# Sums of the activations for the Strassen-like gate products: taken from the x of the q and k stage instead of loaded again per head

## The chip, the cores and the metric

One core of a Trainium2 chip. The metric is the device time of one execution in microseconds; the median of several runs is compared. The engines' names here are those of the profile: PE is TensorE's matrix multiplication and PEld its weight load, DVE is VectorE, ACT is ScalarE, POOL is GpSimd, SP is SyncE, whose queue issues most of the DMAs.

## What is computed

One layer of an encoder trunk, 512 positions of width 1024, all in float32. The part that matters here is the first half:

```python
h = rmsnorm(x, g_pre_mix)                       # (512, 1024)
q, k, v, g, u, sv, a_ret, a_sgu = split(h @ w_in, ...)
y_ret = (layernorm(retention(rotary(q), rotary(k), v)) * silu(g)) @ w_ret_o   # 4 heads, both directions
y_sgu = (gelu(u) * (w_spatial . layernorm(gelu(sv)) + b_spatial)) @ w_sgu_o
x = x + rmsnorm((sigmoid(a_ret) * y_ret + sigmoid(a_sgu) * y_sgu) @ w_out, g_post_mix)
# then a gated MLP with a convolution of width 3, and its norm and residual
```

## The kernel before

**Precision.** Every large product is made of three matmuls. Each operand is split in a high part, a rounded copy made on ACT, and a low part, a subtraction on DVE (`split`, lines 76 to 78); `mm3` (lines 166 to 169) multiplies high by high, high by low and low by high.

**Weights.** All matrices lie in one array of 146 blocks of 128x1024. `w_get` hands out the next unit and issues the loads of those ahead; a load goes into a `raw` buffer, of which there are 4, and its split into two of 9 slots (tag `w4`). A load on SP's queue waits until its raw buffer is free, and a split waits until PE has finished with an older slot.

**The x of q and k.** `load_x(k)` (line 187) loads the k-th of eight 128x512 slices of the transposed x into a scratch buffer (tag `tmp`, 6 of them), and ACT writes its high part, scaled by the norm's gain; `x_low` makes the low part on DVE. The loop at line 205 does this for k = 0 to 7, each time followed by the 24 matmuls of that slice, into eight PSUM banks. High and low parts of all eight slices stay in SBUF until the gates are done.

**Heads.** After the evacuation of q and k, and tables for decay and rotary, the loop at line 557 goes over four heads. Groups of v, sv and g (`t_group`) run on PE between a head's own steps: `k_rows` transposes k and writes `kt`, which is split into `kz`; `scores` makes `sm`; `states` needs kz and makes `st`; `values` makes `o` from sm, st and `qx`, then copies each piece of o out (ACT), takes its mean and variance (DVE, L467 and L468), the inverse root on POOL (`rsqrt`, L233 and L236), and normalizes o (DVE, L473). `prep(h + 1)` makes the next head's q, k and qx. `g_evac` multiplies o by the gate (L524) and transposes it on PE (L514).

**The forms.** The products for u and both gates use seven half-size products instead of eight per pair of blocks (`Pair`, line 590). On the side of the activations they need sums and differences of two slices of x, k and k + 4, and of their two halves in position. `x_forms(h)` (line 536), called once per head, loads both slices again, scales them on ACT (L541), and forms four sums of 128x256 on POOL (L534); `x_form_parts` splits the results one head later into `sh` and `sl`. On the side of the weights, `w_form` makes the sums on DVE (L141, L142) and POOL (L143, L145).

**Order and buffers.** Each engine's instructions stand in one fixed order, chosen before the launch by a scheduler that follows the program's order and a model of when operands and buffers are free; an engine waits at the head of its queue. 74 blocks of 128x512 (tag `blk`) hold everything that lives for some time: x, the forms, q, k, v, o and the rest.

Of the kernel before, what the change touches and what calls it, by code (L numbers as in the profile page):

```python
# [11 lines left out]
F32R = mybir.dt.float32r  # L12
AF = mybir.ActivationFunctionType
ALU = mybir.AluOpType
# [20 lines left out]
PRE, FFNG, LNG, LNB = 0, 8, 16, 24  # L35
# [5 lines left out]
def tile_block(ctx: ExitStack, tc, xT, x, wall, par, cs, decay, wsp, bsp, gpost, gffn, out):  # L41
    nc = tc.nc
# [5 lines left out]
    def nm(s):  # L48
        uid[0] += 1
        return f"{s}_{uid[0]}"  # L50

    def blk(dt=F32, n="blk", shape=(P, S)):
        return sb.tile(list(shape), dt, tag="blk", bufs=NBLK, name=nm(n))

    def tmp(n="tmp", shape=(P, S)):
        return sb.tile(list(shape), F32, tag="tmp", bufs=6, name=nm(n))

    def halves(n):
        return [blk(n=n), blk(n=n)]
# [10 lines left out]
    def copy(o, i):  # L70
        nc.scalar.activation(out=o, in_=i, func=AF.Copy)  # L71

    def as32(t):
        return t.bitcast(F32)

    def split(hi, lo, src):
        copy(hi, src)
        nc.vector.tensor_sub(lo, src, as32(hi))  # L78
# [20 lines left out]
    def raw_tile():  # L99
        return sb.tile([P, 1024], F32, tag="raw", bufs=4, name=nm("raw"))  # L100
# [4 lines left out]
    def w_block(i):  # L105
        raw = raw_tile()
        resident = RES0 <= i < RES1 or i >= NW - RES_DOWN
        if i > 0:
            nc.sync.dma_start(raw, wall[i])
        if resident:  # L110
            hi, lo = [], []
            for c in range(2):
                h_, l_ = blk(F32R, "wh"), blk(F32R, "wl")
                split(h_, l_, raw[:, c * S : (c + 1) * S])
                hi.append(h_)
                lo.append(l_)
        else:
            hi, lo = slot("wh"), slot("wl")
            if i == 0:
                pieces = [slice(0, P), slice(P, S), slice(S, 2 * S)]  # L120
                for f in pieces:
                    nc.sync.dma_start(raw[:, f], wall[i, :, f])
                    (nc.vector.tensor_copy if f.start == 0 else copy)(hi[:, f], raw[:, f])
                for f in pieces:
                    nc.vector.tensor_sub(lo[:, f], raw[:, f], as32(hi[:, f]))
            else:
                split(hi, lo, raw)
        return hi, lo

    def w_form(form, i):  # L130

        if form == "B11":
            a, b = raw_tile(), raw_tile()
            nc.sync.dma_start(a, wall[i])
            nc.sync.dma_start(b, wall[i + 1])
            w_raw["B11"], w_raw["B12"] = a[:, :S], a[:, S:]
            w_raw["B22"], w_raw["B21"] = b[:, :S], b[:, S:]
        elif form == "T1":
            t = raw_tile()
            w_raw["T1"], w_raw["T2"], w_raw["T3"], w_raw["T4"] = t[:, :S], t[:, S:], w_raw["B12"], t[:, S:]  # L140
            nc.vector.tensor_add(w_raw["T1"], w_raw["B11"], w_raw["B12"])  # L141
            nc.vector.tensor_add(w_raw["T3"], w_raw["B12"], w_raw["B22"])  # L142
            nc.gpsimd.tensor_tensor(out=w_raw["T2"], in0=w_raw["T1"], in1=w_raw["B22"], op=ALU.add)  # L143
        elif form == "T4":
            nc.gpsimd.tensor_tensor(out=w_raw["T4"], in0=w_raw["T2"], in1=w_raw["B21"], op=ALU.add)  # L145
        w = slot("wf", 16)
        split(w[:, :S], w[:, S:], w_raw[form])
        return w[:, :S], w[:, S:]

    def w_size(u):  # L150
        return 2 if u[0] == "blk" else 1

    def w_get(look=LOOK):

        i = w_pos[0]
        w_pos[0] += 1
        room = 2 * look + (2 if units[i][0] == "blk" else 0)
        n = sum(w_size(u) for u in units[i : w_pos[1]])
        while w_pos[1] < len(units) and (w_pos[1] <= i or n + w_size(units[w_pos[1]]) <= max(room, 9 if look == LOOK else 0)):
            u = units[w_pos[1]]  # L160
            w_ready[w_pos[1]] = w_block(u[1]) if u[0] == "blk" else w_form(*u)
            w_pos[1] += 1
            n += w_size(u)
        return w_ready.pop(i)

    def mm3(o, ah, al, bh, bl, start, stop):
        nc.tensor.matmul(o, ah, bh, start=start, stop=False)  # L167
        nc.tensor.matmul(o, ah, bl, start=False, stop=False)  # L168
        nc.tensor.matmul(o, al, bh, start=False, stop=stop)  # L169
# [12 lines left out]
    def col(i):  # L182
        return part[:, i : i + 1]

    xh, xl = [], []

    def load_x(k):
        t = tmp("xT")
        nc.sync.dma_start(t, xT[k])
        h_, l_ = blk(F32R, "xh"), blk(F32R, "xl")  # L190
        nc.scalar.activation(out=h_, in_=t, func=AF.Copy, scale=col(PRE + k))
        xh.append(h_)
        xl.append(l_)
        return t

    def x_low(k, t):
        nc.vector.scalar_tensor_tensor(
            out=xl[k], in0=t, scalar=col(PRE + k), in1=as32(xh[k]), op0=ALU.mult, op1=ALU.subtract
        )


    qk = [ps() for _ in range(8)]
    for _ in range(WARM):
        nc.tensor.matmul(qk[7][:, 0 : 2 * P], w16[:, 0:P], w16, start=True, stop=True)
    for k in range(KD):
        xt = load_x(k)
        if k:
            x_low(k, xt)
        wh, wl = w_get(1 if k < 4 else LOOK)
        if k == 0:  # L210
            x_low(k, xt)
            for a, b in ((wh, xh), (wl, xh), (wh, xl)):
                for m in range(8):
                    nc.tensor.matmul(  # L214
                        qk[m], a[:, m * P : (m + 1) * P], b[0], start=a is wh and b is xh, stop=False
                    )
            continue
        for m in range(8):
            c = slice(m * P, (m + 1) * P)
            mm3(qk[m], wh[:, c], wl[:, c], xh[k], xl[k], False, k == KD - 1)  # L220

    ident = const("ident", [P, P])
    make_identity(nc, ident)
# [2 lines left out]
    wst = const("wst", [P, S])  # L226
# [12 lines left out]
    for t in range(NT):  # L239
        for n in range(2):  # L240
            xt = blk(n="x0")
            nc.sync.dma_start(xt, x[t, :, n * S : (n + 1) * S])
            nc.scalar.activation(
                out=xt, in_=xt, func=AF.Square, accum_out=ss[:, 4 * n + t : 4 * n + t + 1]
# [18 lines left out]
    for c in range(19, 1, -2):  # L263
        v.scalar_tensor_tensor(
            out=lc, in0=lc, scalar=1.0 / c, in1=lb, op0=ALU.add, op1=ALU.mult
# [4 lines left out]
        out=lg, in0=lc, scalar=-2.0, in1=lg, op0=ALU.mult, op1=ALU.add  # L270
# [5 lines left out]
    for m in range(8):  # L276
        t = blk(n="qkraw")
# [15 lines left out]
        )  # L293
    rbc = const("rbc", [P, S])
    copy(rbc, rb)
    cosr, sinr = halves("cs")
    nc.sync.dma_start(cosr, cs[0])
    nc.sync.dma_start(sinr, cs[1])
# [226 lines left out]
        transposed([o_sb[t, nh] for t in range(NT)], ogh, ogl)  # L525

    T0, T1 = slice(0, 256), slice(256, 512)  # L530
    forms = {n: [] for n in ("S1", "S2", "S3", "S4")}

    def g_op(o, a, b, op):
        nc.gpsimd.tensor_tensor(out=o, in0=a, in1=b, op=op)  # L534

    def x_forms(k):

        a, b = blk(n="xa"), blk(n="xb")
        for t, j in ((a, k), (b, k + 4)):
            nc.sync.dma_start(t, xT[j])  # L540
            nc.scalar.activation(out=t, in_=t, func=AF.Copy, scale=col(PRE + j))  # L541
        s_ = blk(n="xs")
        g_op(s_[:, T0], a[:, T1], b[:, T1], ALU.subtract)
        g_op(s_[:, T1], s_[:, T0], a[:, T0], ALU.subtract)
        g_op(a[:, T0], a[:, T0], a[:, T1], ALU.subtract)
        g_op(a[:, T1], b[:, T0], s_[:, T1], ALU.add)
        return s_, a

    def x_form_parts(k, s12, s34):
        for names, s_ in (("S1", "S2"), s12), (("S3", "S4"), s34):  # L550
            h_, l_ = blk(F32R, "sh"), blk(F32R, "sl")
            split(h_, l_, s_)
            for n, t in zip(names, (T0, T1)):
                forms[n].append((h_[:, t], l_[:, t]))


    for h in range(H):
        gen = t_group()
        k_rows(h)
        sm = scores(h)  # L560
        acc = next(gen)
        st = states(h)
        next(gen)
        if h + 1 < H:
            prep(h + 1)
        if h:
            x_form_parts(h - 1, *xf)
        xf = x_forms(h)
        values(h, sm, st)
        for _ in gen:  # L570
            pass
        (v_evac, sv_evac, sv_evac, g_evac)[h](acc, (1, 0, 1, 0)[h])
    for acc in t_group():
        pass
    x_form_parts(3, *xf)
    sv_norm()
    g_evac(acc, 1)

# [129 lines left out]
    for j in range(KD // 2):  # L708
        for o, t in gated_pair(ogh, ogl, late if j == 0 else None):
            b = blk(n="r")  # L710
# [5 lines left out]
    for j in range(KD // 2):  # L716
        for i, (o, t) in enumerate(gated_pair(yh, yl)):
            v.tensor_mul(t, o, t)
            nc.gpsimd.tensor_tensor(out=t, in0=t, in1=r[2 * j + i], op=ALU.add)
            h_, l_ = blk(F32R, "mh"), blk(F32R, "ml")  # L720
# [158 lines left out]
    for i in range(NF):  # L879
        cc = []  # L880
        for s_ in range(2):
            e = 2 * i + s_
            o = early_o[e] if e < EARLY else f_block(h2h, h2l, KD)
# [6 lines left out]
    for t in range(NT):  # L890
        q = small("q", 2, 4)
        z = sb.tile([P, 1088], F32, tag="w4", bufs=9, name=nm("z"))[:, :D]
        for n in range(2):
            f = slice(n * S, (n + 1) * S)
            o = dn_.finish(t, n)
# [4 lines left out]
        for i, (a, b) in enumerate(((0, 512), (512, 768), (768, 1024)) if t == NT - 1 else ((0, 512), (512, 1024))):  # L900
            v.scalar_tensor_tensor(
                out=z[:, a:b], in0=z[:, a:b], scalar=sc, in1=x1[t][a // S][:, a % S : a % S + b - a],
# [99 lines left out]
```

## Time and profile before

| | us |
|---|---|
| median of 3 runs | 851.79 (851.08 to 853.01) |
| the profiled execution | 853.29 |
| its span, first to last instruction | 851.5 |
| PE busy | 838.2 (98%) |
| DVE busy | 539.2 (63%) |
| ACT busy | 376.0 (44%) |
| POOL busy | 84.1 (10%) |

The stages, from the timeline of PE: the q and k products run to 53 us, the first group of v to 76, head 0 from 76 to 105, head 1 to 135, head 2 to 164, head 3 to about 202, the last group and the gate's transposes to 225; then u and the two gates to about 440, the output product, the MLP and its down projection. The mean granted clock of TensorE is 0.997. In a line of a timeline the columns are start and duration in us, engine, line, operation, what is written and read, shapes, and in brackets the idle time before it and what ended that.

### The profile page before, as it was taken

The numbers are of one execution on the slowest core, as the hardware profiler recorded it, in microseconds if no ns is written. First come the engines' busy times: TensorE is split into PE (matmuls) and PEld (weight loads), VectorE is DVE, ScalarE is ACT, GpSimd is POOL, SyncE is SP. The second block draws the span as 40 slices with busy tenths as digits, with TensorE's granted clock in tenths as the row PEclk, the third lists the DMA queues.
The fourth block names the chain that finished last, engine by engine and source line by source line (L and its number), as shares of the span: only waits on it lengthen the run. The fifth ranks groups of instructions, "written<-read, shape, count | busy, mean of one in ns | idle before, by whom it ended". The sixth has DMA issues, their size and how long they took to land.

```text
span 851.5 us, 11261 instructions
## 1 busy us (share of the span) xinstructions
PE 838.2 (98%) x4444; PEld 721.1 (85%) x4444; DVE 539.2 (63%) x829; ACT 376.0 (44%) x603; POOL 84.1 (10%) x91
## 2 busy tenths in 40 slices
PE   8999999999999999999999999999999999999996
PEld 6888888877899999999988898888888888888885
DVE  5478798776698677767755766656666666322404
ACT  5435446654565434444444564444444444211301
POOL 0010202121221111032210100000000000000000
PEclk9999999999999999999999999999999999999999
DMA  8633232220223223222456032223232322222202
GB/s 289 236 111 100 99 99 75 83 91 26 87 99 125 100 99 99 99 75 102 148 168 251 1 107 100 94 96 99 99 99 99 100 99 100 95 93 88 95 1 99
DMA packets 28278, 89.97 MB, mean 106 GB/s; under 512 B 3201, under 2 KB 3841, under 8 KB 28225
## 3 DMA queue, kind: packets, MB, share of 16 engines
q1 hardware_dynamic: 27072, 86.91, 29.9%
q0 software_dynamic: 432, 1.32, 0.6%
q10 hardware_dynamic: 720, 1.02, 0.3%
q8 instruction: 35, 0.57, 0.3%
q14 instruction: 19, 0.15, 0.1%
HBM read 87.14 MB, written 2.10 MB: 105 GB/s over the span
## 4 chain that ended last, share of the span: by engine, by line
PE 93%; DVE 3%; POOL 1%; DMA 1%; ACT 1%; issue 1%; SPq 0%; POOLq 0%; DVEq 0%; ACTq 0%
PE ps L167 15%; PE ps L168 15%; PE ps L169 15%; PE ps L604 14%; PE ps L751 6%; PE ps L749 6%; PE ps L750 6%; PE ps L389 4%; PE ps L390 4%; PE ps L391 4%; PE ps L674 1%; PE ps L214 1%; DMA raw<-wall 1%; DVE wl L78 1%; PE ps L514 0%
## 5 line engine op out<-in xcount | busy, mean ns | idle before, releaser
L78 DVE TENSOR_TENSOR wl<-raw,wh 128x1024 fp32r<-128x1024 f32 (+1 forms) x131 | 150.7, 1160 | 166.0 <-PE ps L168 79.6
L71 ACT ACTIVATE wh<-raw 128x1024 fp32r<-128x1024 f32 (+2 forms) x133 | 129.1, 982 | 93.0 <-PE ps L751 45.3
L169 PE MATMUL ps<-h2h,wl 128*128 128x512 f32 (+1 forms) x384 | 142.3, 371 | 0.0
L168 PE MATMUL ps<-h2l,wh 128*128 128x512 f32 (+1 forms) x384 | 142.2, 371 | 0.0
L167 PE MATMUL ps<-h2h,wh 128*128 128x512 f32 (+1 forms) x384 | 142.2, 372 | 0.0
L71 ACT ACTIVATE wf<-raw 128x512 fp32r<-128x512 f32 x84 | 50.8, 627 | 80.7 <-issue 30.2
L167 PEld LDWEIGHTS ps<-h2h,wh 128*128 128x128 f32 x384 | 72.1, 188 | 12.8 <-ACT h2h L815 0.3
L169 PEld LDWEIGHTS ps<-h2h,wl 128*128 128x128 f32 x384 | 72.3, 188 | 12.5
L168 PEld LDWEIGHTS ps<-h2l,wh 128*128 128x128 f32 x384 | 72.2, 188 | 12.3
L78 DVE TENSOR_TENSOR wf<-raw,wf 128x512 fp32r<-128x512 f32 x84 | 64.3, 782 | 26.9 <-ACT wf L71 26.8
L389 PE MATMUL ps<-wh,xh 128*128 128x512 f32 x192 | 75.0, 391 | 0.0
L390 PE MATMUL ps<-wl,xh 128*128 128x512 f32 x192 | 74.9, 390 | 0.0
L391 PE MATMUL ps<-wh,xl 128*128 128x512 f32 x192 | 74.8, 390 | 0.0
L604 PE MATMUL ps<-sh,wf 128*128 128x256 f32 x384 | 72.5, 280 | 0.0
L749 PE MATMUL ps<-wh,fh 128*128 128x512 f32 x176 | 68.5, 389 | 0.0
L750 PE MATMUL ps<-wl,fh 128*128 128x512 f32 x176 | 68.5, 389 | 0.0
L751 PE MATMUL ps<-wh,fl 128*128 128x512 f32 x176 | 68.5, 389 | 0.0
L858 ACT ACTIVATE cv<-ps,part 128x512 f32<-128x512 f32 x44 | 34.3, 780 | 75.9 <-PE ps L169 75.9
L604 PEld LDWEIGHTS ps<-sh,wf 128*128 128x128 f32 x384 | 60.7, 188 | 0.5 <-ACT u L71 0.2
L604 PE MATMUL ps<-xh,wf 128*128 128x256 f32 x288 | 54.6, 281 | 0.0
L604 PE MATMUL ps<-sl,wf 128*128 128x256 f32 x192 | 53.6, 279 | 0.0
L768 POOL TENSOR_TENSOR qr<-qs,nhalf 128x1 f32<-128x1 f32 x12 | 6.6, 552 | 398.1 <-DVE qs L765 398.1
(238 smaller groups left out, 1578.2 us busy)
## 6 DMA issues: line engine op xcount, KB each, us to landing
raw<-wall SPq DMA_DIRECT2D x145, 512.0 KB, 3.3
x<-x SPq DMA_DIRECT2D x16, 256.0 KB, 6.2
xT<-xT SPq DMA_DIRECT2D x8, 256.0 KB, 5.7
xa<-xT SPq DMA_DIRECT2D x4, 256.0 KB, 3.6
xb<-xT SPq DMA_DIRECT2D x4, 256.0 KB, 3.9
out<-z SPq DMA_DIRECT2D x4, 256.0 KB, 2.0
out<-z ACTq DMA_DIRECT2D x3, 256.0 KB, 2.0
cs<-cs SPq DMA_DIRECT2D x2, 256.0 KB, 4.0
```

Of the source, the lines that this page charges most:

```text
L71: nc.scalar.activation(out=o, in_=i, func=AF.Copy)
L78: nc.vector.tensor_sub(lo, src, as32(hi))
L167: nc.tensor.matmul(o, ah, bh, start=start, stop=False)
L168: nc.tensor.matmul(o, ah, bl, start=False, stop=False)
L169: nc.tensor.matmul(o, al, bh, start=False, stop=stop)
L389: nc.tensor.matmul(acc[t], xh[k][:, c], wh[:, f], start=k == 0, stop=False)
L390: nc.tensor.matmul(acc[t], xh[k][:, c], wl[:, f], start=False, stop=False)
L391: nc.tensor.matmul(acc[t], xl[k][:, c], wh[:, f], start=False, stop=k == KD - 1)
L604: nc.tensor.matmul(o, w_[:, c], a_, start=first and k == n == 0, stop=k == 3 and n == 2, skip_group_check=True,)
L749: nc.tensor.matmul(o, ah, bh, start=k == 0, stop=False)
L750: nc.tensor.matmul(o, ah, bl, start=False, stop=False)
L751: nc.tensor.matmul(o, al, bh, start=False, stop=k == self.nk - 1)
```

## The change

It makes the forms from the slices that the q and k loop has loaded anyway. `x_scaled` writes a scaled copy of a loaded slice (`xg`) on ACT, two rounds of the loop after its load, the last two behind the loop; the slice's scratch buffer stays in use until then. The four `x_forms`, with sums on DVE instead of POOL and with their splits, follow directly behind the q and k loop, ahead of the program's evacuation of q and k. The eight loads inside the heads and the sums on POOL are gone. The 16 blocks of the split forms are so in use from there to the end of the gates.

Two more edits: `hold` takes one of the four raw buffers at the start and gives it back when ACT has copied 16 columns of the low part of slice 1 into it, in the round k = 2. And one column of `rbc` is copied into `wst`, so that the load of w_spatial (line 647) comes after that copy.

```diff
+    def x_scaled():
+        k = len(xg)
+        xg.append(blk(n="xg"))
+        nc.scalar.activation(out=xg[k], in_=xts[k], func=AF.Copy, scale=col(PRE + k))
+
+    hold = raw_tile()
+    nc.vector.memset(hold[:, 0:16], 0.0)
...
+    xts = []
     for k in range(KD):
         xt = load_x(k)
+        xts.append(xt)
         if k:
             x_low(k, xt)
+        if k == 2:
+            copy(hold[:, 0:16], as32(xl[1])[:, 0:16])
         wh, wl = w_get(1 if k < 4 else LOOK)
...
+        if k > 1:
+            x_scaled()
         for m in range(8):
             c = slice(m * P, (m + 1) * P)
             mm3(qk[m], wh[:, c], wl[:, c], xh[k], xl[k], False, k == KD - 1)
+    x_scaled()
+    x_scaled()
+
+    T0, T1 = slice(0, 256), slice(256, 512)
+    forms = {n: [] for n in ("S1", "S2", "S3", "S4")}
+
+    def x_forms(k):
+        a, b = xg[k], xg[k + 4]
+        s_ = blk(n="xs")
+        nc.vector.tensor_sub(s_[:, T0], a[:, T1], b[:, T1])
+        nc.vector.tensor_sub(s_[:, T1], s_[:, T0], a[:, T0])
+        nc.vector.tensor_sub(a[:, T0], a[:, T0], a[:, T1])
+        nc.vector.tensor_add(a[:, T1], b[:, T0], s_[:, T1])
+        for names, s_ in (("S1", "S2"), s_), (("S3", "S4"), a):
+            h_, l_ = blk(F32R, "sh"), blk(F32R, "sl")
+            split(h_, l_, s_)
+            for n, t in zip(names, (T0, T1)):
+                forms[n].append((h_[:, t], l_[:, t]))
+
+    for k in range(4):
+        x_forms(k)
...
     rbc = const("rbc", [P, S])
     copy(rbc, rb)
+    copy(wst[:, 0:1], rbc[:, 0:1])
...
-    def g_op(o, a, b, op):
-        nc.gpsimd.tensor_tensor(out=o, in0=a, in1=b, op=op)
-
-    def x_forms(k):
-        a, b = blk(n="xa"), blk(n="xb")
-        for t, j in ((a, k), (b, k + 4)):
-            nc.sync.dma_start(t, xT[j])
-            nc.scalar.activation(out=t, in_=t, func=AF.Copy, scale=col(PRE + j))
-        s_ = blk(n="xs")
-        g_op(s_[:, T0], a[:, T1], b[:, T1], ALU.subtract)
-        ...
-        return s_, a
-
-    def x_form_parts(k, s12, s34):
-        ...
     for h in range(H):
...
-        if h:
-            x_form_parts(h - 1, *xf)
-        xf = x_forms(h)
         values(h, sm, st)
...
     for acc in t_group():
         pass
-    x_form_parts(3, *xf)
     sv_norm()
     g_evac(acc, 1)
```

More of the change, by code (lines that the diff above doesn't have):

```diff
@@ L183, in col @@
         return part[:, i : i + 1]
-    xh, xl = [], []
+    xh, xl, xg = [], [], []
     def load_x(k):
@@ L525, in g_evac @@
         transposed([o_sb[t, nh] for t in range(NT)], ogh, ogl)
-    T0, T1 = slice(0, 256), slice(256, 512)
-    forms = {n: [] for n in ("S1", "S2", "S3", "S4")}
-    def g_op(o, a, b, op):
-        nc.gpsimd.tensor_tensor(out=o, in0=a, in1=b, op=op)
-    def x_forms(k):
-        a, b = blk(n="xa"), blk(n="xb")
-        for t, j in ((a, k), (b, k + 4)):
-            nc.sync.dma_start(t, xT[j])
-            nc.scalar.activation(out=t, in_=t, func=AF.Copy, scale=col(PRE + j))
-        s_ = blk(n="xs")
-        g_op(s_[:, T0], a[:, T1], b[:, T1], ALU.subtract)
-        g_op(s_[:, T1], s_[:, T0], a[:, T0], ALU.subtract)
-        g_op(a[:, T0], a[:, T0], a[:, T1], ALU.subtract)
-        g_op(a[:, T1], b[:, T0], s_[:, T1], ALU.add)
-        return s_, a
-    def x_form_parts(k, s12, s34):
[L550 to L554, printed above, removed]
     for h in range(H):
```

## The prediction

> **What bounds the kernel now.** I read the page's engine table and slices first, then the start-to-start steps of TensorE's (PE's) matmuls for gaps, then the waits of PE, and last the engine timelines where PE waited.
>
> ```profile
> PE 838.2 (98%) x4444; PEld 721.1 (85%) x4444; DVE 539.2 (63%) x829; ACT 376.0 (44%) x603; POOL 84.1 (10%) x91
> ```
>
> PE is busy 98% of the span and the change leaves its 4444 matmuls alone, so it can only gain or lose at PE's gaps. In steady state a 512-wide matmul starts 0.227 us after the last and a 256-wide one 0.118 us. Summing every start-to-start step above these gives 11.6 us of gaps in all: 5.6 us before 13.2 us of the span, while the first weights land, and almost all the rest between 171 and 225 us. The waits of PE name them (engine, line and tile, releaser: total us, times, longest):
>
> ```profile
> PE ps L214 <- ACT wh L71: 2.4, 2, 1.7
> PE ps L514 <- DVE o L524: 1.7, 4, 0.9
> ...
> PE ps L169 <- DVE kz L78: 0.8, 1, 0.8
> PE ps L167 <- ACT kz L71: 0.7, 1, 0.7
> ```
>
> The two kz rows are the place that the change touches: states(3) waits for the split of the last head's decayed keys. In PE's timeline (start, duration):
>
> ```profile
> 171.32 0.39 PE L391 MATMUL ps<-wh,xl 128*128 128x512 f32 x1
> 172.45 0.39 PE L167 MATMUL ps<-vh,kz 128*128 128x256 f32 x1 [0.73 <-ACT kz L71]
> 172.67 0.28 PE L168 MATMUL ps<-vl,kz 128*128 128x256 f32 x1
> 173.78 0.39 PE L169 MATMUL ps<-vh,kz 128*128 128x256 f32 x1 [0.83 <-DVE kz L78]
> 174.01 0.28 PE L167 MATMUL ps<-vh,kz 128*128 128x256 f32 x1
> ```
>
> Steps 1.13, 0.22, 1.11 and 0.23 us where 0.23, 0.12, 0.12 and 0.12 are normal: 2.1 us lost. What made kz late stands in the timelines of ScalarE (ACT), GpSimd (POOL) and VectorE (DVE), one fence each:
>
> ```profile
> 159.95 0.71 ACT L541 ACTIVATE xa<-xa,part 128x512 f32<-128x512 f32 x1
> ...
> 161.17 0.36 ACT L71 ACTIVATE o<-ps 128x256 f32<-128x256 f32 x1
> ```
>
> ```profile
> 163.79 0.74 POOL L534 TENSOR_TENSOR xa<-xb,xs 128x256 f32<-128x256 f32 x1
> 164.62 0.20 POOL L233 TENSOR_SCALAR rs<-mv 128x4 f32<-128x4 f32 x1
> ```
>
> ```profile
> 163.24 0.18 DVE L468 BATCH_NORM_AGGREGATE mv<-bs 128x2 f32<-128x6 f32 x1
> 165.95 1.39 DVE L473 TENSOR_SCALAR o<-o,mv,orstd 128x256 f32<-128x256 f32 x4 [2.52 <-POOL orstd L236]
> ...
> 171.09 0.64 DVE L372 TENSOR_TENSOR kt<-ps,zt 128x512 f32<-128x512 f32 x1
> ```
>
> The copies of o stood behind the two scalings of x on ACT (159.95 to 161.17); the mean and variance were ready at 163.42, but the rsqrt on POOL stood behind the four sums until 164.62; DVE then did L473, a weight split, the sv statistics and only at 171.09 kt, which the kz split needs.
>
> **What is removed.** From each head: 8 loads in all, two scalings on ACT, four sums on POOL, and two copies and two subtractions of the splits one head later. For head 3: ACT's xa and xb took 1.2 us ahead of the first o copy; POOL's queue cost 164.62 - 163.43 = 1.2 us more. DVE gets to L473 2.4 us sooner at least, and the two sl subtractions (0.68 each) queued there at 156.95 are gone as well. If the whole 2.4 us carries through, kt comes at 168.7 and kz is done when PE asks for it at 171.5; **the 2.1 us go**. Next late would be values(3): its sm split ended at 180.22 for PE's 180.55 and its state split at 180.81 for 181.26, margins of 0.33 and 0.45, after 7.1 us of unbroken DVE work from kz. PE will be there 2.1 us sooner and DVE 2.4, so it just holds. Were only POOL's 1.2 us gained, the gain would be 1.2 + 0.33 = 1.5. Ends: 0 (kt stays behind the same work) and 2.1. I take 2.0.
>
> The second gap is the gating of the first half (L524 before the transposes L514), 2.3 us from 195.5 to 200.3. There L473 started at 191.02, 3.60 us after DVE fell idle, again with POOL's sums in front of the rsqrt, and with xa and xb of 1.2 us on ACT. It would end before 189 instead of at 192.4. What is late next is the weight split wl, whose wh comes from ACT at 191.59 after a wait for PE: it starts at 191.65 rather than 192.32, and all that follows on DVE (L141, L142, L524) 0.7 us sooner. The first L524 still meets POOL's L143:
>
> ```profile
> 194.35 1.79 POOL L143 TENSOR_TENSOR raw<-raw,raw 128x512 f32<-128x512 f32 x1 [3.36 <-DVE raw L141]
> ...
> 194.91 2.98 DVE L524 TENSOR_TENSOR o<-o,g 128x512 f32<-128x512 f32 x3
> ```
>
> Three of 0.68 took 2.98 there, and the change leaves L143 as it is, so most of this gap stays: ends 0 and 2.3, I take 0.7. The last gap, near 222 us, waits for gates made after all forms are done: 0.
>
> **What is added.** Eight scalings on ACT (0.71 each by L541), eight split copies (0.62 by sh), sixteen sums and eight subtractions (0.68 by sl) on DVE, all before 53 us. No 256-wide two-input operation on DVE is in the trace: an 8-wide one takes 0.17, a 512-wide one 0.69, so between 0.17 and 0.69, by interpolation 0.43. ACT gets 5.7 + 5.0 = 10.7 us and DVE 6.9 + 5.4 = 12.3 us. Room, by the windows (PE, PEld, DVE, ACT, POOL busy):
>
> ```profile
> 15.00:53.00 38.00, 38.00 (x170) 31.45 (x169) 18.95 (x43) 18.40 (x35) 2.83 (x5) 1.00 0.64 229
> 53.00:76.00 23.00, 23.00 (x108) 19.14 (x107) 19.07 (x28) 9.28 (x13) 0.00 (x0) 1.00 0.29 93
> ```
>
> DVE would be at 31 of 38 us and ACT at 29 of 38. The last x lands at 31.54, so the last forms can be done by about 38; PE's next need of DVE is the evacuation of q and k from 49.29. Cover: 38 to 49.29 less 2.6 us of weight splits, 8.7 us. Cost nothing. On ACT, x_scaled stands among the weight copies; weights for k = 2 were ready at 13.8 and are used at 20.5, so 0.71 or 1.42 more is hidden, and k = 1 has xl at 12.61 for 15.3.
>
> The held raw buffer moves the fourth weight load in SyncE's queue, and xT3 behind it, from 4.83 to the release of the first buffer near 9.7. Without these two loads, 768 KB, the queue that ran at 408 to 420 GB/s then has about what it can do until 13.4, when that block landed before; it is used at 26. The copy that ends the hold waits on ACT for xl[1] (12.61), and ahead of wh of k = 2 or 3 that is 1.3 us into 6 us of lead. Loads landed in the order of issue, so those in front should gain nothing: 0, with ends of -1.0 (TensorE waits 3.1 us there for the first block's pieces) and +0.6 (one ACT operation of 0.71 ahead of a piece). The w_spatial load now waits for rbc (about 55 us instead of 28); it is used at 223, and the weight loads behind it on SyncE come every 5.4 us. Nothing.
>
> Buffers: the forms now hold 16 of the 74 blocks through all heads, where before 0, 4, 8 and 12 were held with three scratch ones. Counting live blocks in program order gives 76 at most, in prep(2) during head 1: two writes of qx wait for blocks that values(1) frees. In the trace values(1) runs on PE from 119.5 to 123.9 and qx of head 2 is written at 126.2 and used at 149.7, so the wait ends by itself; without that cover DVE would stand for up to 3 us, against 4.7 us that kt of head 2 (137.4) has until PE's 142.1.
>
> **Sum.** -2.0 - 0.7 + 0 + 0 = -2.7 us: 853.29 of the profiled execution becomes 850.6. The median of the runs is 851.79, 1.5 less than the profiled one; carried over, **849.1**.
>
> **The clock of the start.** PE's granted clock was 0.50 between 10 and 12 us, and eight matmuls that started between 9.67 and 12.66 took 1.5 us more than usual in sum. Whether a shift in the first landings takes such a window away or adds one, no row tells; I allow 1.5 either way in the range. [...]
>
> **Rivals.**
> 1. *The stall only moves.* In the last head DVE is busy without a break from 173 to 181, margin 0.33 us; if the new order of DVE's queue leaves kt or sm where it was, PE waits there instead, and only the 0.7 is gained: 851.1. For: DVE busy 30.3 of 37 us in the stage from 165 to 202. Against: 2.4 us leave the two queues ahead of it. 0.12.
> 2. *The forms come late (slower).* If DVE does the 12.3 us of forms only behind the evacuation of q and k, it has 3.9 us idle in 53 to 76 and 3.5 us of margin at kz of head 0 (split done at 79.9, used at 83.4): 12.3 - 7.4 = 4.9 us on PE, less 2.7: 854.0. It decides once over 7.4 us of forms are undone at 49.3. For: DVE, at 31 of 38 us, has little left in that stage. Against: the last inputs are there at 34. 0.22.
> 3. *More goes.* Both late gaps vanish and the start gains its slow window or about as much: -2.1 - 2.3 - 1.5 = -5.9, 845.9. For: DVE has its L473 done over 3 us sooner. Against: L143 stays in front of L524. 0.14.
> 4. *The held buffer does nothing.* Loads land in order, so I hold this for likely; it is part of the forecast.
>
> **How the numbers follow.** The forecast has 0.52. A measurement of this kernel can tell about 0.2%, 1.7 us, from no change. The forecast's own range is 847.6 to 850.6 (1.5 either way for the start); of its 0.52, 0.08 fall within 0.2%, as do 0.10 of rival 1. Faster 0.44 + 0.02 + 0.14 = 0.60, same 0.08 + 0.10 = 0.18, slower 0.22. The range reaches down to 846.0 and up to 853.5, leaving out half of rival 3 and over half of rival 2.
>
> **What would show it.** Right: no sum on POOL between 97 and 190, L473 of head 3 waiting under 2 us, PE's two kz waits gone, the L514 wait about 1 us, 16 short DVE operations between 15 and 45 us. Wrong: a new PE wait at sm, st or the q and k evacuation, or a first block that lands elsewhere than at 8.3 us.

## The result: slower by 0.9%, through a wait that the prediction did not list

The changed kernel takes 858.34 us (857.63 to 860.48), the kernel before 851.43 over four runs: ratio 1.0086 [1.0059, 1.0113]. In the larger sets of runs beside the experiments (18 to 23) the kernel before has medians of 852.28 to 852.94. Predicted were 849.1 us and a gain. The profiled execution took 857.87 us, with a span of 856.1.

The engine table of the changed kernel's page (busy us, share of the span, instructions):

```profile
PE 838.8 (98%) x4444; PEld 722.1 (84%) x4444; DVE 547.2 (64%) x846; ACT 377.5 (44%) x605; POOL 70.1 (8%) x75
```

PE has the same work as before, 838.8 against 838.2 us, so the time lies again in its gaps. Its waits in the changed kernel (line and tile, releaser: total us, times, longest):

```profile
PE ps L327 <- POOL rstd L276: 6.9, 1, 6.9
...
PE ps L555 <- DVE o L565: 0.3, 1, 0.3
```

The two kz rows are gone, and the row of the gate's transposes (L514 before, L555 now) has gone from 1.7 to 0.3. The first row is new. L327 are eight small matmuls that spread `rstd`, the inverse root of the mean square of x, over all partitions, right behind the q and k products. This is the code (lines of the changed kernel 281 to 288; the matmuls follow the evacuation of q and k):

```python
            xt = blk(n="x0")
            nc.sync.dma_start(xt, x[t, :, n * S : (n + 1) * S])
            nc.scalar.activation(
                out=xt, in_=xt, func=AF.Square, accum_out=ss[:, 4 * n + t : 4 * n + t + 1]
            )
    nc.vector.tensor_add(ss[:, :NT], ss[:, :NT], ss[:, NT : 2 * NT])
    rstd = const("rstd", [P, NT])
    rsqrt(rstd, ss[:, :NT], 1.0 / D, NT)
```

The same windows as in the prediction, and the new hole (us, then PE, PEld, DVE, ACT, POOL busy, granted clock, DMA share, GB/s):

```profile
15.00:53.00 38.00, 37.78 (x167) 30.97 (x165) 28.48 (x64) 22.75 (x36) 0.00 (x0) 1.00 0.63 222
53.00:62.00 9.00, 2.31 (x10) 2.21 (x10) 5.17 (x10) 6.67 (x18) 3.06 (x5) 0.66 0.40 142
```

Up to 53 us PE is as full as before, with DVE at 28.5 of 38 us. Then PE works 2.31 of 9 us.

**Where the time went.** The table sums PE's start-to-start steps, each less the usual step of its shape, where the excess is over 60 ns (us):

| PE time lost in | before | changed |
|---|---|---|
| start, to 17 us | 4.9 | 4.3 |
| end of q and k, 45 to 70 us | 0.1 | 8.6 |
| the four heads, 70 to 188 us | 2.4 | 0.3 |
| first gate half, to 214 us | 2.3 | 0.45 |
| the rest | 2.1 | 2.6 |
| sum | 11.8 | 16.3 |

In the row of the heads all but 0.3 us lies in the last head, from kz to values(3). The gain was there, 3.9 us in the two places that the prediction named, and 8.5 us were lost at a third. Of the 8.6 us, 7.1 are the step from the last q and k matmul to the first of L327, and 1.5 are eleven matmuls behind it at half clock. The sum rises by 4.5 us where the spans differ by 4.6. That the medians differ by 6.9 is because the profiled execution of before was slow for its kernel, and that of the changed kernel fast.

**Why rstd is late.** SP's queue (start, duration of the issues, line, tile, number), before:

```profile
32.67 0.33 SPq L109 DMA_DIRECT2D raw<-wall  x1
33.05 4.24 SPq L242 DMA_DIRECT2D x<-x  x8
38.12 11.23 SPq L109 DMA_DIRECT2D raw<-wall  x3
```

and in the changed kernel:

```profile
32.12 11.46 SPq L109 DMA_DIRECT2D raw<-wall  x3
43.64 3.90 SPq L282 DMA_DIRECT2D x<-x  x8
49.43 4.80 SPq L109 DMA_DIRECT2D raw<-wall  x2
```

The eight loads of x for the norm stand behind three weight loads instead of one, counted from the load of the last slice for q and k. The weight loads at 37.56 and 43.26 wait for a raw buffer, one per 5.5 us, so the x loads are issued 10.6 us later and land between 47.82 and 53.25 us rather than between 37.01 and 43.16. From there the chain of waits goes on to PE:

```profile
52.56 0.24 PE ps L169
52.82 1.06 ACT wh L71
53.88 3.06 ACT x L283 x10
56.94 0.48 ACT qkraw L71
57.42 0.62 ACT x L283 x2
58.06 0.17 DVE ss L286
58.32 0.20 POOL rs L273
58.60 1.06 POOL rstd L276
59.70 2.08 PE ps L327 x8
```

The last x landed at 53.25, yet its square was done at 58.06. ACT's timeline shows why: after two of the eight squares it stands 2.28 us at a weight copy that waits for PE, with the other six queued behind it.

```profile
50.35 0.19 ACT L283 ACTIVATION_READ_ACCUMULATOR x<-x 128x1 f32 x1
52.82 1.06 ACT L71 ACTIVATE wh<-raw 128x1024 fp32r<-128x1024 f32 x1 [2.28 <-PE ps L169]
53.78 0.61 ACT L283 ACTIVATE x<-x 128x512 f32<-128x512 f32 x1
```

### The profile page after: what moved, and what is told of

It reads as the page before. It is cut to its first block, busy times and chain, and to the rows that moved or that the text cites. A ratio compares the mean times of both kernels' runs of the same rounds, so it can differ in the third digit from the quotient of the medians.

```text
span 856.1 us, 11249 instructions
## 1 busy us (share of the span) xinstructions
PE 838.8 (98%) x4444; PEld 722.1 (84%) x4444; DVE 547.2 (64%) x846; ACT 377.5 (44%) x605; POOL 70.1 (8%) x75
## 4 chain that ended last, share of the span: by engine, by line
PE 94%; DVE 3%; ACT 1%; DMA 1%; issue 0%; POOL 0%; SPq 0%; POOLq 0%; DVEq 0%; ACTq 0%
PE ps L167 15%; PE ps L168 15%; PE ps L169 15%; PE ps L612 11%; PE ps L758 6%; PE ps L759 6%; PE ps L757 6%; PE ps L430 5%; PE ps L431 5%; PE ps L432 5%; DVE wf L78 2%; DMA raw<-wall 1%; PE ps L227 1%; PE ps L682 1%; PE ps L555 0%
## 5 line engine op out<-in xcount | busy, mean ns | idle before, releaser
L78 DVE TENSOR_TENSOR wf<-raw,wf 128x512 fp32r<-128x512 f32 x84 | 67.3, 818 | 26.8 <-ACT wf L71 26.5
L612 PEld LDWEIGHTS ps<-xh,wf 128*128 128x128 f32 x288 | 45.5, 188 | 0.4
```

What stands on the lines that cost most here:

```text
L612: nc.tensor.matmul(o, w_[:, c], a_, start=first and k == n == 0, stop=k == 3 and n == 2, skip_group_check=True,)
```

## The experiments

Three theories were open. *Place*: the x0 blocks come after the blocks of the forms in the program, in the same pool, and so their loads come later in SP's queue. *Load*: DVE and ACT have too much to do ahead of 53 us. *Hold*: the held raw buffer delays the queue.

**e1: the forms behind rstd.** The four calls are moved behind the rsqrt of x's norm.

```diff
-    for k in range(4):
-        x_forms(k)
     ...
     rsqrt(rstd, ss[:, :NT], 1.0 / D, NT)
+    for k in range(4):
+        x_forms(k)
```

> The changed kernel with the four calls of x_forms moved behind the loop that loads and squares x for the norm. Theory 1 (place: x for the norm is loaded late because its blocks come after those of the forms in program order): its loads start near 33 us, not 43.6, the 6.9 us wait of the broadcast of rstd is gone, and with what follows it (the transposes and first matmuls at half clock) 8.7 us go: 858.3 - 8.7 = 849.6 by the changed kernel's runs, 847.3 by the spans, so 847 to 850. Theory 2 (load: DVE and ACT simply have too much to do before 53 us): the wait stays, now for the evacuation of q and k, 856 to 859. Theory 3 (the held buffer delays the loads): 856 to 859.

Measured: 856.34 us, ratio 1.0041 [1.0026, 1.0057]. The x loads go out at 31.71 and the wait at rstd is gone, but the expected time is missed. PE now waits at the same matmuls for something else; the wait, then DVE's timeline:

```profile
PE ps L328 <- ACT qkraw L71: 4.3, 1, 4.3
```

```profile
55.67 0.69 DVE L78 TENSOR_TENSOR sl<-xg,sh 128x512 fp32r<-128x512 f32 x1 [0.15 <-ACT sh L71]
56.28 2.48 DVE L320 COPY qkraw<-ps 128x512 f32<-128x512 f32 x4
```

The forms last until 56.3 us, and the evacuation of q and k stands behind them on DVE and ACT; until it frees a PSUM bank, PE has none for L328. This is rival 2 of the prediction, in place and mechanism. So with the norm's x in the blocks' pool, the forms cost PE time on both sides of rstd.

**e2: x for the norm from another pool.** One word of the changed kernel: the norm's x takes the scratch pool of xT, which has 6 buffers.

```diff
-            xt = blk(n="x0")
+            xt = tmp("x0")
```

> The changed kernel with the place of the forms in the program as it is; only the eight tiles of x for the norm come from the scratch buffers (tag tmp) instead of the blocks (tag blk) that the forms use. Theory 1: the order inside the pool is what holds the loads back, so they start near 32 us and the time is that of the experiment with the forms moved, 847 to 850. Theory 2 and theory 3: no change, 856 to 859. Were it the place in the program as such and not the pool: 856 to 859 as well.

Measured: 849.53 us, ratio 0.9957 [0.9941, 0.9973]: faster than before by 3.4 us at the medians, and 8.8 under the changed kernel. SP's queue and PE's waits:

```profile
26.49 2.51 SPq L282 DMA_DIRECT2D x<-x  x3
30.88 0.33 SPq L109 DMA_DIRECT2D raw<-wall  x1
32.16 2.78 SPq L282 DMA_DIRECT2D x<-x  x5
```

```profile
PE ps L227 <- ACT wh L71: 2.4, 2, 1.2
PE ps L213 <- DVE raw L208: 1.0, 1, 1.0
PE ps L555 <- DVE o L565: 0.3, 1, 0.3
```

Every form is still made ahead of 53 us, with the same work on DVE and ACT, and no wait is left between 17 and 214 us that is over 0.3. *Load* falls: DVE was at 31.25 of 38 us in that window, more than in the changed kernel, and cost PE nothing.

**e3: the changed kernel without the held buffer**, and **e4: the kernel before with it.** In e3 the first and the last pair of these lines are taken out of the changed kernel; in e4 they are put into the kernel before.

```diff
     hold = raw_tile()
     nc.vector.memset(hold[:, 0:16], 0.0)
...
         if k == 2:
             copy(hold[:, 0:16], as32(xl[1])[:, 0:16])
```

> The changed kernel without the held raw buffer, its memset and its copy. Theory 1 and theory 2: the wait for rstd stays at 5 to 7 us, 856 to 859. Theory 3: the wait is gone, 847 to 851.

> The kernel before with the held raw buffer alone. Theory 1 and 2: 851.4, within 1 either way; the start moves by what the landings of the first block move. Theory 3: slower by 5 to 7, 856 to 858.

Measured: e3 858.85 us, ratio 1.0062 [1.0048, 1.0077], with the wait unchanged:

```profile
PE ps L323 <- POOL rstd L272: 6.9, 1, 6.9
```

e4 853.27 us, ratio 1.0006 [0.9994, 1.0018]. The held buffer does nothing that these runs can tell, with or without the rest. *Hold* falls.

**e5: the kernel before with late x.** Nothing of the change; each x0 block first gets one column from the high part of weight block 10, so that its load waits for them.

```diff
             xt = blk(n="x0")
+            copy(xt[:, 0:1], as32(w_ready[10][0])[:, 0:1])
             nc.sync.dma_start(xt, x[t, :, n * S : (n + 1) * S])
```

> The kernel before, with nothing of the change but late loads of x for the norm: each of the eight tiles first gets one column of the high part of weight block 10, so that the loads stand behind three weight loads in SyncE's queue, where the changed kernel has them, and not behind one. Theory 1 (the late loads are the price): the loads start near 43.6 us, TensorE waits 5 to 7 us for rstd, and with the half clock behind it the kernel is slower by 6 to 8.7: 859 to 862 beside 852.9. If the price lies in the work of the forms: 852 to 854.

Measured: 858.7 us, ratio 1.0066 [1.0052, 1.0080]. Late x alone, without any form in front, gives a wait at the same matmuls and most of the loss there, 5.2 of the 8.6 us. The loads come at the changed kernel's times (issued from 43.52, landed 47.76 to 53.30), but the wait is 3.3 us, not the 5 to 7 expected, and the time is just under the range:

```profile
PE ps L288 <- POOL rstd L236: 3.3, 1, 3.3
```

ACT's timeline in e5, then the sum of squares on DVE:

```profile
48.47 1.05 ACT L71 ACTIVATE wh<-raw 128x1024 fp32r<-128x1024 f32 x1
49.49 0.63 ACT L244 ACTIVATE x<-x 128x512 f32<-128x512 f32 x1
```

```profile
54.55 0.16 DVE L247 TENSOR_TENSOR ss<-ss 128x4 f32<-128x4 f32 x1 [0.55 <-ACT x L244]
```

Here no weight copy that waits for PE stands among the squares, and ss comes at 54.55 instead of 58.06, from the same landings. So the 6.9 us of the changed kernel are about 3.3 of late loads and 3.5 of ACT's order behind them. The second part is a comparison of two traces; no run changed that order alone. In the profiled execution the time rose more than the wait because half clock cost 1.8 us behind it and 1.6 more behind the kz gap (last section).

**e6: two forms ahead of x, two behind rstd.**

```diff
-    for k in range(4):
+    for k in range(2):
         x_forms(k)
     ...
     rsqrt(rstd, ss[:, :NT], 1.0 / D, NT)
+    for k in range(2, 4):
+        x_forms(k)
```

> The changed kernel with two of the four x_forms ahead of the loads of x for the norm and two behind. Theory 1: these loads stand behind one weight load fewer, 5.4 us sooner, near 38 us; the wait for rstd of 6.9 falls to 0 to 1.5, and the last forms end near where they end when all stand ahead (50 us), so the evacuation of q and k waits less than the 4.3 us of the experiment with all behind: 849 to 854. If the order were all or nothing: 856 to 859.

Measured: 853.95 us, ratio 1.0014 [1.0004, 1.0023]. The x loads go out at 37.84 us, early enough that rstd makes nobody wait; the evacuation is late by less than in e1:

```profile
PE ps L330 <- ACT qkraw L71: 2.7, 1, 2.7
```

With none, two and four forms ahead of x in the program, the first x load is issued at 31.71, 37.84 and 43.64 us; one weight load more stands ahead of it each time. No buffer is short: by the count of the program 53 of the 74 blocks are taken with the last x0. So it is the fixed order of the queue that puts these loads late, and by e2 it is the shared pool that decides it. That the planner hands out a pool's blocks in the program's order, and so can't place an x0 load ahead of the writers of earlier blocks, is inferred from these four positions.

**e7: only the sums to DVE.** The kernel before, with `g_op` on `nc.vector`.

```diff
-        nc.gpsimd.tensor_tensor(out=o, in0=a, in1=b, op=op)
+        nc.vector.tensor_tensor(out=o, in0=a, in1=b, op=op)
```

> The kernel before with the sums of x_forms on DVE instead of POOL, everything else in its place in the heads. What took the 2.1 us of kz and most of the 2.3 us of the gate out of the changed kernel: if it is POOL's queue ahead of the rsqrt, both gaps shrink here as well, by 2.5 to 4: 849 to 850.5 beside 852.9. If ACT's scalings and the splits in the heads matter as much, or DVE's 1.7 us more for each head takes the place of POOL's, less than half: 851.5 to 854.

Measured: 851.48 us, ratio 0.9983 [0.9973, 0.9993]. The kz waits go, and others take their place in values(3):

```profile
PE ps L169 <- DVE sm L78: 0.5, 1, 0.5
PE ps L168 <- DVE st L78: 0.2, 1, 0.2
PE ps L167 <- ACT sm L71: 0.2, 1, 0.2
```

In the heads PE loses 2.26 us instead of 2.44: rival 1 of the prediction, the stall that moves. At the gate it loses 0.96 instead of 2.27. So taking the sums off POOL alone brings over half of the gate gap and next to nothing in the heads; the time lies between the two ranges, at the edge of the second.

**e8: e2 without the held buffer and without the copy into wst.**

```diff
-    hold = raw_tile()
-    nc.vector.memset(hold[:, 0:16], 0.0)
...
-        if k == 2:
-            copy(hold[:, 0:16], as32(xl[1])[:, 0:16])
...
-    copy(wst[:, 0:1], rbc[:, 0:1])
```

> The changed kernel with x for the norm in the scratch buffers, and without the held raw buffer and without the copy into wst. If these two do nothing: 848 to 851 as with them, PE's only waits at the start. If the held buffer brings something at the start: 1 to 2 us slower than with it.

Measured: 847.62 us, ratio 0.9942 [0.9926, 0.9958], the fastest kernel of the study and a little under the range, 4.9 us under the one before by the ratio. Its interval overlaps that of e2. Their profiles differ mainly at the start, where PE lost 1.7 and 3.4 us; e9, whose start is written as that of e2, lost 5.9 there, so that this is no mark of the edit.

**e9: e2 with the sums in front on POOL.**

```diff
-        nc.vector.tensor_sub(s_[:, T0], a[:, T1], b[:, T1])
+        nc.gpsimd.tensor_sub(s_[:, T0], a[:, T1], b[:, T1])
```

and the three operations below it in the same way.

> The kernel of the run in which x for the norm takes the scratch pool, and in it the sixteen sums of the forms on POOL instead of DVE, at the same place in the program. If DVE's load ahead of 53 us costs nothing once x for the norm is early (theory 1, the place in the pool of blocks): no change against that run, 847 to 851 us, and no wait of PE at rstd or at the evacuation of q and k. If the load of DVE is still a part of it (theory 2): under 847 us. If POOL's sums stand ahead of the rsqrt of the x norm (POOL's queue): a wait of PE at rstd of 2 us or more, 852 to 856 us. Sums at 0.74 us on POOL are 11.8 us in all.

Measured: 848.69 us, ratio 0.9956 [0.9940, 0.9971]; no wait at rstd or the evacuation. Which engine makes the sums in front does not matter to what these runs can tell.

**e10: only the loads in front.** x_scaled runs in front as in e2; sums (POOL) and splits stay in the heads, on `xg` instead of loaded blocks.

```diff
-        a, b = blk(n="xa"), blk(n="xb")
-        for t, j in ((a, k), (b, k + 4)):
-            nc.sync.dma_start(t, xT[j])
-            nc.scalar.activation(out=t, in_=t, func=AF.Copy, scale=col(PRE + j))
+        a, b = xg[k], xg[k + 4]
```

> The same kernel, but only the scaled copies of x are made in front; the sums (on POOL) and the splits stay in the heads, where the kernel before has them. So the heads lose the eight loads and the eight scalings on ACT, and keep the sums on POOL and the splits one head later. If POOL's queue in front of the rsqrt made the key split of the last head late: the two kz waits and the gate gap stay at half their size or more (1 to 2 us of kz, 1 to 2.3 us of the gate), 850 to 853 us. If the scalings on ACT ahead of the copies of o made it late: both gaps go as in the changed kernel, 847 to 850 us.

Measured: 850.19 us, ratio 0.9978 [0.9966, 0.9990]. It does not tell its two theories apart, because the queue of POOL changed with the scalings:

```profile
160.27 0.20 POOL L274 TENSOR_SCALAR rs<-mv 128x4 f32<-128x4 f32 x1 [20.66 <-DVE mv L510]
...
168.95 0.74 POOL L249 TENSOR_TENSOR xs<-xg,xg 128x256 f32<-128x256 f32 x1
```

The four sums now stand behind the rsqrt. The gate gap falls to 0.45 us as in the changed kernel, but in the heads PE still loses 1.7 of 2.4 us, mostly at st of the last:

```profile
PE ps L168 <- DVE st L78: 0.7, 1, 0.7
```

kt is early here (166.74 against 171.09 before), but the sums now run beside DVE's work for kz, sm and st. DVE's timeline in e10, then the same operations in e2, where no sum is left in the heads:

```profile
169.89 1.22 DVE L78 TENSOR_TENSOR kz<-kt,kz 128x512 fp32r<-128x512 f32 x1
171.03 1.22 DVE L376 SCALAR_TENSOR_TENSOR dec<-dd,lg,dec 128x512 f32<-128x512 f32 x1
...
178.87 0.68 DVE L78 TENSOR_TENSOR st<-ps,st 128x512 fp32r<-128x512 f32 x1
```

```profile
167.21 0.68 DVE L78 TENSOR_TENSOR kz<-kt,kz 128x512 fp32r<-128x512 f32 x1
167.81 0.74 DVE L375 SCALAR_TENSOR_TENSOR dec<-dd,lg,dec 128x512 f32<-128x512 f32 x1
...
174.75 0.68 DVE L78 TENSOR_TENSOR st<-ps,st 128x512 fp32r<-128x512 f32 x1
```

The operations between are the same in both. The kz split and the decay took 0.54 and 0.48 us longer beside POOL's sums, and from kz to st it is 8.98 us instead of 7.54. That 1.4 us is more than the 0.7 us that PE waits for st; the heads lose 0.34 us in e2, 1.69 in e10. By these traces POOL's sums can cost in two ways, by standing ahead of the rsqrt and by slowing DVE; no run took the second away alone.

## Why the prediction was wrong

**The step that failed** is the one that ends "Cost nothing", under "What is added". The load that it reckoned was about right: sixteen sums at 0.42 us against 0.43 by interpolation; in e2 DVE was at 31.25 of 38 us against 31 and ACT at 29.60 against 29. (The changed kernel has 28.48 and 22.75, as the evacuation and six of the eight squares moved past 53 us.) But its cover ran from 38 us to "PE's next need of DVE", and that was given as the evacuation of q and k from 49.29. The stage has a second need: x is loaded again, squared, summed and inverted for the norm, and PE waits for the result in the same place. This chain was nowhere in the working. It had ended at 45.5 in the trace before (rstd, 44.47 and 1.04), with 7.7 us to spare until PE used it at 53.17, and the change moved it by 14.1 us: 10.6 in SP's queue, the rest mostly on ACT. The prediction followed the instructions that the change moves; it did not ask which loads that the change leaves alone come behind the new blocks in the program, and take their place in the queue from that.

**The forms also came later** than "by about 38": DVE had the last sl at 49.29 to 49.98, since sh on ACT and the sums on DVE wait for each other in turn (the pairs of forms at 42.1, 44.6, 46.8 and 47.7 us on ACT, with gaps of 0.4 to 1.6 between). So the cover of 8.7 us was hardly there. It was just enough: in e2 the last sl ends at 50.04 and the evacuation on DVE (49.96 to 53.58) makes PE wait for nothing. In e1, where the squares on ACT come first, the forms last until 56.3, and rival 2's wait comes, 4.3 us. In the changed kernel ACT copies its first bank only from 56.84 on, behind squares and not behind forms, and PE's longer wait for rstd covers that.

**What held.** *kz*: 2.0 us taken, 2.1 gained; values(3), which was to "just hold", holds in the changed kernel, e2, e8 and e9, which lose 0.1 us or less from kz to there, and is late in e7 and e10, where DVE has more to do. *Gate*: 0.7 taken of bounds 0 to 2.3, 1.8 gained. POOL's L143, which was to keep most of the gap, started 0.56 us ahead of the first three gate products before (194.35 against 194.91), which took 2.98 us; now it starts 1.28 us ahead (198.33 against 199.61), and they take 2.41. *The held buffer*: 0 taken, nothing in e3 and e4; the first block's last piece landed at 8.22 us where 8.3 was said. *The wst copy* and *the buffers*: no wait of PE shows them. *The clock of the start*: PE's start loss ranged from 1.7 to 5.9 us over the profiles of all kernels, so an allowance of 1.5 either way was rather narrow.

**Two rows misread.** The trace of the kernel before does have two-input operations of 256 columns on DVE (L627, 0.42 us), so nothing had to be interpolated. And the split of kz of head 0 ended at 80.35 and not at 79.9, which leaves rival 2 0.4 us less room.

With the failed step mended, the sum by the prediction's own terms would have been: -2.1 - 1.8 at the two gaps and +8.5 at rstd, +4.6 in all, as the spans have it. With that wait avoided, e2 gives 849.53 us beside 849.1 predicted. That the two lie so close is partly luck: the gaps brought 3.9 us where 2.7 were taken, and the kernel before took 852.94 beside e2, not 851.79.

## What to carry to other kernels

A block that is allocated earlier in the program can delay a load that comes after it in the same pool, though no buffer is short (x is issued from 43.64 us in the changed kernel, from 26.49 with another pool in e2): after an edit, list every load behind it in the program that shares a pool or a queue, and follow each to PE. For a stage with a dense PE, list all of the things that PE waits for at its end, not only the engine that gets more work. And in a queue whose head waited for buffers, one weight load per 5.5 us, a shift of two places became 10.6 us.

## What the runs showed of the hardware

A wait of PE can cost more than its length, since half clock may follow it. After the 6.9 us of the changed kernel the granted clock was 0.50 from 55.8 to 62.7 us, 6.8 us in all; after 4.3 us in e1 also 6.8 (54.3 to 61.2); after 3.3 in e5 and 2.7 in e6, 3.4 us (56.4 to 59.8 and 56.1 to 59.5). The matmuls in it lost 1.5, 2.4, 1.8 and 1.7 us. The length of the wait alone does not decide it: in e3 the same 6.9 us were followed by 10.2 us of half clock, in which the matmuls lost 3.0 (the mean granted clock of that execution was 0.989, of the changed kernel's 0.993). These lengths are one, two and three times 3.41 us. Nor must PE wait 3.41 us for it: in e6 it waited 2.7.

The changes of the granted clock also lie on a grid in time. In the kernel before they come at 9.50, 12.91 and 849.18 us, 1 and 245 times 3.4133 us apart; in the changed kernel at 8.04, 11.45, 55.83, 62.65 and 854.54, 1, 13, 2 and 232 times; in e5, of those near the two gaps, at 56.39, 59.80, 179.27 and 182.68, 1, 35 and 1 times. Counted from the start of the span the grid lies elsewhere in each of the three, its first point at 2.67, 1.21 and 1.78 us. So the same gap can cost more or less by where it falls. The kz gap of the kernel before stands in e5 too. Cut into windows of this grid it lies in two of them in the kernel before, and in one in e5, followed by the next (columns as in the windows above):

```profile
169.93:173.34 3.41, 2.29 (x10) 1.42 (x8) 2.95 (x10) 1.56 (x2) 1.20 (x2) 1.00 0.35 136
173.34:176.75 3.41, 2.97 (x18) 2.67 (x19) 3.41 (x6) 1.94 (x3) 0.00 (x0) 1.00 0.09 18
```

```profile
175.86:179.27 3.41, 1.84 (x11) 1.22 (x10) 2.95 (x7) 2.03 (x3) 1.20 (x2) 1.00 0.01 2
179.27:182.68 3.41, 3.41 (x12) 2.93 (x12) 3.41 (x6) 1.89 (x3) 0.00 (x0) 0.50 0.41 105
```

PE was busy 2.29 and 2.97 of 3.41 us in the two windows of the first, and the clock stayed at 1.00. In the one window of the second it was busy 1.84, and the next ran at 0.50, which cost 1.5 us. In the kernel before, half clock also followed the window from 6.09 to 9.50 us, with PE busy for 1.66 us, and in the changed kernel those from 4.63 to 8.04 and from 52.41 to 55.82, with 1.16 and 0.37. It did not follow the one from 847.72 to 851.13 of the changed kernel, with 1.75. Every other window at full clock of these two profiles, from the first of these to the end of PE's work, had PE busy for 2.29 us or more, and full clock followed. So in these profiles it was a window with PE busy for about half of it or less that brought half clock, not only an idle one; the 1.75 (full) and e5's 1.84 (half) give no sharp limit.

The second is POOL beside DVE. In e10 and e9 two-input operations of both engines took longer where they overlapped: DVE's 128x512 split 1.22 us instead of 0.68, POOL's 128x256 sum up to 1.65 instead of 0.74 (e9, in front: the sum began at 32.63, inside a 128x1024 split on DVE that began at 32.46 and took its usual 1.22). In e10 the 0.54 us more of the split is under one sum's 0.74. Why the two slow each other no trace shows.
